# Gate norm, convolution, GELU and the product with up moved from the w_down stage into the Strassen stage, and four k tiles of w_out moved to its second part

## The chip, the cores and the metric

The kernel runs on one NeuronCore of one Trainium2 chip. The metric is the device time of one execution in microseconds, shown as the median of the runs, lower being better. The engines are TensorE (PE, with its weight loads as PEld), VectorE (DVE), ScalarE (ACT), GpSimd (POOL) and SyncE (SP). SP issues nearly all DMAs. Each engine works through its own queue strictly in order, and a semaphore wait of one instruction holds up all that stands behind it in that queue.

## The reference

One decoder layer on a (1, 512, 2048) float32 input. Three groups of attention heads feed one output projection; then a gated MLP with a causal depthwise convolution of width 3; then a gated per-layer embedding. The part that matters here:

```python
h = h + jnp.concatenate([oa, ob, oc], axis=-1) @ w_out[i]
c = rmsnorm(h, ffn_norm[i])
h = h + conv_ffn(c, w_gate[i], w_up[i], conv_w[i], conv_b[i], w_down[i])
e = rmsnorm(h, ple_norm[i])
h = h + jax.nn.sigmoid(e @ w_ple_gate[i]) * (p[i] @ w_ple_proj[i])

def conv_ffn(x, w_gate, w_up, conv_w, conv_b, w_down):
    hg = x @ w_gate                                  # (512, 5632)
    hg = causal_depthwise_conv(hg, conv_w, width=3) + conv_b
    return (jax.nn.gelu(hg, approximate=True) * (x @ w_up)) @ w_down
```

## The kernel before, in words

Every float32 matmul is done as three fp32r products. An operand is split into a high part (a cast on ACT, names ending in h) and a low part (a subtraction on DVE, names ending in l), and PE multiplies high by high, high by low and low by high. Weights come by DMA into `raw` tiles (three buffers), and `split_into` (lines 162 and 163 of the kernel) makes `wh` on ACT and `wl` on DVE (four buffers each).

The stages in order of time, each a list of groups that `run_groups` works through:

1. The input projection w_in, with the attention of the three head groups running beside it as background generators.
2. w_out in two parts. The four column blocks c = 0..3 (512 columns each) are first multiplied over 12 of the 16 k tiles (`order1`), and the result is added to x in `evac_o1` (line 1066). Then the four blocks are multiplied over the last four k tiles, and `evac_o2` (line 1071) adds these into `h` on DVE. The first part runs while the last attention unit is finished.
3. When a block c of `h` is complete, `operands(c)` transposes it on PE (line 1107), scales it on ACT (`T`, line 1108), and forms the seven Strassen operands of its k tiles on DVE (`st`, `sl`, lines 1116 and 1126) and ACT (`sh`, line 1121). `stats_store(c)` sums the squares on ACT (line 509) and stores `h` to DRAM. At the same time PE multiplies the second part of w_out for the next block and then w_ple_proj, the small product of the embedding (`evac_pp`).
4. The Strassen stage: 22 blocks of 256 columns of w_gate and 22 of w_up, taken in turn. A `Pair` is one such block. It takes seven products P1 to P7, each 8 k tiles by 3 matmuls of 256 columns, on PE lines 343 to 345. DVE forms weight differences (`T`, lines 238 to 248) and the `wl` splits and adds up results (lines 364, 367, 371); ACT makes the `wh` splits and copies results out of PSUM. `store_pair` then stores the two result tiles of the pair (128 x 512 each) to DRAM (`gu`).
5. w_down over 44 k tiles, in two passes: columns 0 to 1023, then 1024 to 2047. In the first pass `gated_load` loads the gate and up tiles of a k tile back, and `gated` makes its hidden tile: `z` = gate times the norm's scale on DVE (line 1207), the first tap with bias on ACT (line 1208), two more taps on DVE (lines 1210, 1213), GELU on ACT (line 1216), the product with up on DVE (line 1218). `hid_split` then makes `hh` on ACT (line 1227) and `hl` on DVE (line 1229). The 44 hidden tiles stay in SBUF for the second pass, which only splits them again.
6. w_ple_gate, and the output.

What sets the order: the program is recorded in the order in which the Python code calls it, with no scheduler behind it. Between pieces of PE work the code calls `tick()`, which advances every generator in the background list `bg` by one step. There are two ticks in each Strassen product and one after each bank of a group. `advance_split` puts the weight split of a product three places ahead of it. `need` functions run before a group or product and may tick until what they need has been recorded. All 512-column tiles of the background work share one pool of 69 pages; a page is used again when its last reader has finished.

Of the kernel before, what the change touches and what calls it, by code (L numbers as in the profile page):

```python
# [16 lines left out]
P = 128  # L17
# [35 lines left out]
def hybrid_layer_kernel(  # L53
# [142 lines left out]
    class Pair:  # L196


        def __init__(self, w, ct, dst):
            self.w, self.ct, self.dst = w, ct, dst  # L200
# [152 lines left out]
    def evac_product(p_, kind):  # L353
        m = T // 2
        x = p_.x[:, :m]
        if kind == "P1":
            p_.s = [page("ps") for _ in range(2)]
            p_.u = [page("pu") for _ in range(2)]
            p_.s1, p_.s2, p_.s3 = p_.s[0][:, :m], p_.s[0][:, m:], p_.s[1][:, :m]
            ACT.copy(p_.s1, x)  # L360
        elif kind == "P6":
            ACT.copy(p_.s2, x)
        elif kind == "P2":
            DVE.tensor_tensor(p_.u[0][:, :m], p_.y[:, :m], p_.s1, op=ALU.add)
        elif kind == "P7":
            ACT.copy(p_.s3, x)  # L366
            DVE.tensor_tensor(p_.u[1][:, m:], p_.z[:, :m], p_.s3, op=ALU.add)
        elif kind == "P4":
            ACT.copy(p_.u[0][:, m:], x)
        elif kind == "P3":  # L370
            DVE.tensor_tensor(p_.u[1][:, :m], p_.z[:, :m], p_.s2, op=ALU.add)
            bg.append(store_pair(p_))

    def store_pair(p_):
        for c in range(2):
            yield
            yield
            SP.dma_start(p_.dst(p_.ct + c), p_.u[c])
# [706 lines left out]
    def stats_store(c):  # L1085
        for t in range(NT):
            cT.stat(t, c, hp)
            yield
        while state.get("operands", -1) < c:
            yield  # L1090
        for t in range(NT):
            hd[t, c] = dpool.tile([P, NB], F32, tag=name("hd"), name=name("hd"))
            SP.dma_start(hd[t, c], hp[t][c])
        if c == 3:
            yield from cT.finish_gen(True)

# [84 lines left out]
    gd, ud = {}, {}  # L1181

    def pair_dst(d):
        def dst(ct):
            d[ct] = dpool.tile([P, T], F32, tag=name("gu"), name=name("gu"))
            return d[ct]
        return dst

    NC = D_FF // P
    cur = {"kt": -1}  # L1190
    gp = {}

    def gated_load():

        for kt in range(NC):
            while kt > cur["post"] + 2 or kt not in gd or kt not in ud:
                yield
            g, u = page("g"), page("u")
            SP.dma_start(g, gd[kt])
            SP.dma_start(u, ud[kt])  # L1200
            gp[kt] = g, u
            yield

    def gated(kt):
        g, u = gp.pop(kt)
        z = page("z")
        DVE.tensor_tensor(z, g, cT.rb, op=ALU.mult)
        ACT.activation(g, z, AF.Identity, scale=conv_col(2, kt), bias=conv_col(3, kt))  # L1208
        yield
        DVE.scalar_tensor_tensor(  # L1210
            g[:, 1:], z[:, : T - 1], conv_col(1, kt), g[:, 1:], op0=ALU.mult, op1=ALU.add
        )
        DVE.scalar_tensor_tensor(
            g[:, 2:], z[:, : T - 2], conv_col(0, kt), g[:, 2:], op0=ALU.mult, op1=ALU.add
        )
        ACT.activation(g, g, AF.Gelu_apprx_tanh)
        yield
        DVE.tensor_tensor(u, g, u, op=ALU.mult)
        hid_raw[kt] = u
        yield from hid_split(kt)  # L1220

    hid_raw = {}

    def hid_split(kt):
        u = hid_raw[kt]
# [5 lines left out]
        yield  # L1231

    def gated_all():
        for kt in range(NC):
            while kt > cur["kt"] + 4 or kt not in gp:
                yield
            cur["post"] = kt
            bg.append(gated(kt))
            yield
            yield  # L1240
            yield

    def split_all():
        for kt in range(NC):
            while kt > cur["kt"] + 4:
                yield
# [43 lines left out]
    def load_p():  # L1290
        pt = [page("p") for _ in range(2)]
# [16 lines left out]
    def evac_pp(c):  # L1308
        def evac(b, ps):
            t = xtile("b22")[:, :NB] if c < 2 else page("ppe")  # L1310
# [73 lines left out]
    order1 = [0, 1, 2, 3, 8, 9, 10, 11, 4, 5, 6, 7]  # L1384
    for c in range(4):
# [11 lines left out]
        groups.append(Group(2, w_out, krow, [(c * NB, NB)], mk, order1, evac_o1(c), need=need))  # L1397
    for c in range(4):
        need = None
        if c == 0:  # L1400
            need = once(lambda: (drain(units[2]["attn"]), open_xpool(), bg.append(conv_constants())))
        elif c == 2:
            need = once(lambda: bg.append(load_p()))
        groups.append(Group(2, w_out, krow, [(c * NB, NB)], mk, [12, 13, 14, 15], evac_o2(c), need=need))
# [5 lines left out]
    for q in range(NC // 2):  # L1410
        pairs.append(Pair(w_gate, 2 * q, pair_dst(gd)))
        pairs.append(Pair(w_up, 2 * q, pair_dst(ud)))
    order = [(0, "P1")]
    for r in range(len(pairs)):
        if r < len(pairs) - 1:
            order += [(r, "P5"), (r, "P6"), (r, "P2"), (r, "P7"), (r + 1, "P1"), (r, "P4"), (r, "P3")]
        else:
            order.insert(-1, (r, "P5"))
            order.insert(-1, (r, "P6"))
            order += [(r, "P7"), (r, "P2"), (r, "P4"), (r, "P3")]  # L1420
    for r, kind in order:
        if r < len(pairs):
# [5 lines left out]
            if (r, kind) == (len(pairs) - 1, "P6"):  # L1428
                def begin_down():
                    cur["post"] = -1  # L1430
                    bg.extend([gated_load(), gated_all()])
                c.need = begin_down

    for cs in ((0, 1), (2, 3)):
        def need(kts, cs=cs):
            if kts[0] == 0:
                cur["kt"] = -1
                if cs[0]:
                    hid.clear()
# [93 lines left out]
```

## Time and profile before

| | |
|---|---|
| median of 3 runs | 2585.02 us (2583.57 to 2585.78) |
| the profiled execution, its own time | 2583.13 us |
| its span, first to last instruction | 2581.4 us |
| PE busy | 2510.5 us, 97% of the span |
| DVE busy | 1441.8 us, 56% |
| ACT busy | 995.8 us, 39% |
| mean granted PE clock | 0.990 |

The profiled execution's time is 1.7 us above its span. Matmuls are pipelined, so that PE counts as busy whenever one is in flight; how many matmuls were done in a stretch of time says more of PE than its busy share. The stages begin at about 692 us (w_out, first part), 848 us (its second part), 906 us (w_ple_proj), 946 us (Strassen), 1837 us (w_down, first pass), 2147 us (second pass) and 2392 us (w_ple_gate). In the views of waits, "A <- B" says that engine A sat idle before its instruction until instruction B ended.

### The profile page before, as it was taken

To read this page: it belongs to the slowest core of one execution; us is meant where nothing else is said; L and a number is where in the kernel's file an instruction comes from. 1 tells how busy PE (TensorE), PEld (TensorE's weight loads), DVE (VectorE), ACT (ScalarE), POOL (GpSimd) and SP (SyncE) were. 2 spreads that over 40 slices of the span, in tenths; PEclk is the share of its full clock that TensorE was granted. 3 is DMA by queue.
4 is the path that set the end of the run, shared out by engine and by line. 5 is a ranking of instruction groups with operands and counts; after the bars stand their busy time and mean duration, and the time that the engine had idled before them with its cause. 6 is when DMAs were issued, how large, how long until landed. Compare 5 with 4: busy or idle time off the path is not lost.

```text
span 2581.4 us, 36548 instructions
## 1 busy us (share of the span) xinstructions
PE 2510.5 (97%) x14956; PEld 2210.9 (86%) x14956; DVE 1441.8 (56%) x1865; ACT 995.8 (39%) x1450; POOL 131.1 (5%) x232
## 2 busy tenths in 40 slices
PE   9999999999999889999999999999888889999999
PEld 7888898888888779999999999999766667888887
DVE  5253445445553577677777777677666664233433
ACT  5222244344432454444444444444444444222422
POOL 1132300101000000000000000000000000000000
PEclk9999999999999999999999999999899999999999
DMA  5322232232333354444444444444444453334342
GB/s 179 91 82 66 77 89 86 79 100 73 111 101 107 107 172 140 138 125 129 129 145 128 132 123 142 137 127 145 145 133 161 132 167 110 98 98 131 130 136 85
DMA packets 294180, 308.76 MB, mean 120 GB/s; under 512 B 12300, under 2 KB 207861, under 8 KB 294011
## 3 DMA queue, kind: packets, MB, share of 16 engines
q1 hardware_dynamic: 293978, 306.41, 38.6%
q8 instruction: 117, 1.92, 0.3%
q14 instruction: 53, 0.43, 0.1%
q10 hardware_dynamic: 32, 0.01, 0.0%
HBM read 270.70 MB, written 35.66 MB: 119 GB/s over the span
## 4 chain that ended last, share of the span: by engine, by line
PE 85%; DVE 7%; ACT 5%; issue 2%; DMA 0%; SPq 0%; ACTq 0%; DVEq 0%
PE g L313 13%; PE g L315 13%; PE g L314 12%; PE x L345 6%; PE x L343 6%; PE x L344 6%; PE m L345 5%; PE m L343 5%; PE m L344 5%; PE m L314 2%; PE m L315 2%; PE m L313 2%; DVE wl L163 1%; ACT g L1208 1%; ACT wh L162 1%
## 5 line engine op out<-in xcount | busy, mean ns | idle before, releaser
L163 DVE TENSOR_TENSOR wl<-raw,wh 128x1024 fp32r<-128x1024 f32 (+1 forms) x350 | 427.8, 1233 | 528.1 <-ACT wh L162 526.7
L162 ACT CAST wh<-raw 128x1024 fp32r<-128x1024 f32 (+1 forms) x350 | 360.5, 1042 | 537.8 <-PE g L315 385.9
L343 PE MATMUL x<-sh,wh 128*128 128x256 f32 x1408 | 398.8, 283 | 6.9 <-ACT ps L366 5.4
L313 PE MATMUL g<-wh,ah 128*128 128x512 f32 (+2 forms) x1024 | 398.4, 389 | 0.8 <-ACT ah L501 0.8
L345 PE MATMUL x<-sh,wl 128*128 128x256 f32 x1408 | 398.4, 283 | 0.0
L344 PE MATMUL x<-sl,wh 128*128 128x256 f32 x1408 | 397.6, 282 | 0.0
L315 PE MATMUL g<-wh,al 128*128 128x512 f32 (+2 forms) x1024 | 390.0, 381 | 0.0
L314 PE MATMUL g<-wl,ah 128*128 128x512 f32 (+2 forms) x1024 | 388.6, 379 | 0.0
L163 DVE TENSOR_TENSOR wl<-T,wh 128x1024 fp32r<-128x1024 f32 x176 | 215.4, 1224 | 158.3 <-ACT wh L162 158.3
L343 PE MATMUL m<-sh,wh 128*128 128x256 f32 x1056 | 298.1, 282 | 0.0
L345 PE MATMUL m<-sh,wl 128*128 128x256 f32 x1056 | 297.9, 282 | 0.0
L344 PE MATMUL m<-sl,wh 128*128 128x256 f32 x1056 | 297.4, 282 | 0.0
L343 PEld LDWEIGHTS x<-sh,wh 128*128 128x128 f32 x1408 | 268.7, 191 | 7.3 <-ACT ps L366 5.6
L345 PEld LDWEIGHTS x<-sh,wl 128*128 128x128 f32 x1408 | 268.9, 191 | 0.0
L344 PEld LDWEIGHTS x<-sl,wh 128*128 128x128 f32 x1408 | 268.8, 191 | 0.0
L315 PEld LDWEIGHTS g<-wh,al 128*128 128x128 f32 x1024 | 192.8, 188 | 38.9 <-DVE al L502 0.5
L314 PEld LDWEIGHTS g<-wl,ah 128*128 128x128 f32 x1024 | 193.5, 189 | 34.5
L313 PEld LDWEIGHTS g<-wh,ah 128*128 128x128 f32 x1024 | 193.4, 189 | 34.1 <-ACT ah L501 1.2
L162 ACT CAST wh<-T 128x1024 fp32r<-128x1024 f32 x176 | 184.9, 1051 | 64.3 <-PE m L344 61.4
L345 PEld LDWEIGHTS m<-sh,wl 128*128 128x128 f32 x1056 | 200.8, 190 | 0.0
L343 PEld LDWEIGHTS m<-sh,wh 128*128 128x128 f32 x1056 | 200.7, 190 | 0.0
L344 PEld LDWEIGHTS m<-sl,wh 128*128 128x128 f32 x1056 | 200.7, 190 | 0.0
(271 smaller groups left out, 3876.4 us busy)
## 6 DMA issues: line engine op xcount, KB each, us to landing
raw<-in_w_down_dram SPq DMA_DIRECT2D x88, 512.0 KB
raw<-in_w_in_dram SPq DMA_DIRECT2D x82, 512.0 KB
raw<-in_w_gate_dram SPq DMA_DIRECT2D x66, 512.0 KB
raw<-in_w_up_dram SPq DMA_DIRECT2D x66, 512.0 KB
gu<-pu SPq DMA_DIRECT2D x88, 256.0 KB
raw<-in_w_out_dram SPq DMA_DIRECT2D x32, 512.0 KB
raw<-in_w_ple_gate_dram SPq DMA_DIRECT2D x32, 512.0 KB
b<-in_w_gate_dram SPq DMA_DIRECT2D x22, 512.0 KB
```

The source lines that it names most:

```text
L162: ACT.copy(c.h[:, :m], src)
L163: DVE.tensor_tensor(c.l[:, :m], src, c.h[:, :m].bitcast(F32), op=ALU.subtract)
L313: PE.matmul(o, th, ch, start=st, stop=False)
L314: PE.matmul(o, th, cl, start=False, stop=False)
L315: PE.matmul(o, tl, ch, start=False, stop=sp)
L343: PE.matmul(ps, vh[:, k, :], ah, start=st and k == 0, stop=False, skip_group_check=not st)
L344: PE.matmul(ps, vh[:, k, :], al, start=False, stop=False, skip_group_check=not st)
L345: PE.matmul(ps, vl[:, k, :], ah, start=False, stop=k == 7, skip_group_check=not st)
L1208: ACT.activation(g, z, AF.Identity, scale=conv_col(2, kt), bias=conv_col(3, kt))
```

## The change

- The gate tiles no longer go to DRAM. When a gate pair is done, `gate_done` puts two steps for each of its two tiles on a list: `gate_norm` (`z` on DVE and the first tap on ACT) and `gate_conv` (two taps on DVE, GELU on ACT). When an up pair is done, `up_done` adds a step `hidden` for each tile: the product on DVE, and then a store of the finished hidden tile to DRAM (`hid`). The generator `step_all` does one step every four ticks, that is every two products, and one every tick once w_down has begun.
- w_down loads the hidden tile of each k tile from DRAM, in both passes, and splits it; the 44 tiles no longer stay in SBUF. The loads of the first pass begin at the last pair's P7.
- A pair takes one page for its partial sums in place of two.
- w_out: block 0 keeps 12 k tiles in the first part and 4 in the second; blocks 1 to 3 have 8 in each. `stats_store` does its sums and stores after the operands of the block. The tiles of p and the results of w_ple_proj lie in other buffers, and p is loaded one block later.

Three places show how the instructions moved. The first is DVE in the second part of w_out, where the sums of the block's last bank into `h` stand, for which the transposes wait (`st` and `sl` are the Strassen operands of the block before, `wl` a weight split). Before, from the third bank's sum of block 1 on:

```order
L1071 TENSOR_TENSOR h_5948<-g_7062,h_5948 128x512
L1116 TENSOR_TENSOR st_7110<-T_7012 128x512
L1126 TENSOR_TENSOR sl_7114<-T_7013,sh_7090 128x512
L1126 TENSOR_TENSOR sl_7118<-st_7110,sh_7112 128x512
L1116 TENSOR_TENSOR st_7120<-T_7013,st_7084 128x512
L1126 TENSOR_TENSOR sl_7124<-T_7013,sh_7116 128x512
L1126 TENSOR_TENSOR sl_7126<-st_7120,sh_7122 128x512
L163 TENSOR_TENSOR wl_7131<-raw_6948,wh_7130 128x1024
L1071 TENSOR_TENSOR h_5970<-g_7096,h_5970 128x512
```

After the change, the same block:

```order
L1120 TENSOR_TENSOR sl_6937<-st_6931,sh_6933 128x512
L163 TENSOR_TENSOR wl_6944<-raw_6768,wh_6943 128x1024
L163 TENSOR_TENSOR wl_6966<-raw_6816,wh_6965 128x1024
L1065 TENSOR_TENSOR h_5887<-g_6818,h_5887 128x512
L1065 TENSOR_TENSOR h_5922<-g_6852,h_5922 128x512
L1065 TENSOR_TENSOR h_5948<-g_6877,h_5948 128x512
L419 COPY cw_6758<-m_7001 128x88
L163 TENSOR_TENSOR wl_7022<-raw_6850,wh_7021 128x1024
L1065 TENSOR_TENSOR h_5970<-g_6908,h_5970 128x512
```

The operands of block 0 are now all ahead of the four sums of block 1, and only a weight split and a small copy stand between the last two sums.

The second place is DVE in the middle of the Strassen stage, from a sum of P3 on (`L371`) to the next product's difference. Before:

```order
L371 TENSOR_TENSOR pu_9827<-m_9864,ps_9824 128x256
L163 TENSOR_TENSOR wl_10120<-T_10087,wh_10119 128x1024
L248 TENSOR_TENSOR T_10021<-raw_9961,T_10021 128x1024
L163 TENSOR_TENSOR wl_10153<-raw_10027,wh_10152 128x1024
L163 TENSOR_TENSOR wl_10187<-T_10021,wh_10186 128x1024
L364 TENSOR_TENSOR pu_10055<-m_10158,ps_10053 128x256
L238 TENSOR_TENSOR T_10217<-raw_10123,raw_10027 128x1024
```

After the change, at such a place:

```order
L371 TENSOR_TENSOR pu_8845<-m_8720,ps_8683 128x256
L163 TENSOR_TENSOR wl_8980<-T_8947,wh_8979 128x1024
L1196 TENSOR_TENSOR z_8997<-pu_8844,rb 128x512
L248 TENSOR_TENSOR T_8883<-raw_8818,T_8883 128x1024
L163 TENSOR_TENSOR wl_9014<-raw_8889,wh_9013 128x1024
L163 TENSOR_TENSOR wl_9046<-T_8883,wh_9045 128x1024
L1201 SCALAR_TENSOR_TENSOR pu_8844<-z_8997,cw_6758,pu_8844 128x511
L1204 SCALAR_TENSOR_TENSOR pu_8844<-z_8997,cw_6758,pu_8844 128x510
L364 TENSOR_TENSOR pu_9078<-m_9019,ps_8915 128x256
L238 TENSOR_TENSOR T_9081<-raw_8983,raw_8889 128x1024
```

One step of the gate tile now stands between splits, two products apart from the next.

The third place is DVE in the first pass of w_down, two k tiles. Before:

```order
L163 TENSOR_TENSOR wl_18559<-raw_18460,wh_18558 128x1024
L1207 TENSOR_TENSOR z_18574<-g_18480,rb 128x512
L1210 SCALAR_TENSOR_TENSOR g_18480<-z_18574,cw_6938,g_18480 128x511
L1213 SCALAR_TENSOR_TENSOR g_18480<-z_18574,cw_6938,g_18480 128x510
L1218 TENSOR_TENSOR u_18481<-g_18480,u_18481 128x512
L1229 TENSOR_TENSOR hl_18594<-u_18481,hh_18593 128x512
L1207 TENSOR_TENSOR z_18607<-g_18512,rb 128x512
L1210 SCALAR_TENSOR_TENSOR g_18512<-z_18607,cw_6938,g_18512 128x511
L1213 SCALAR_TENSOR_TENSOR g_18512<-z_18607,cw_6938,g_18512 128x510
L1218 TENSOR_TENSOR u_18513<-g_18512,u_18513 128x512
L1229 TENSOR_TENSOR hl_18627<-u_18513,hh_18626 128x512
L163 TENSOR_TENSOR wl_18637<-raw_18472,wh_18636 128x1024
```

After the change:

```order
L163 TENSOR_TENSOR wl_18404<-raw_18275,wh_18403 128x1024
L163 TENSOR_TENSOR wl_18419<-raw_18335,wh_18418 128x1024
L1237 TENSOR_TENSOR hl_18416<-hid_18379,hh_18415 128x512
L1237 TENSOR_TENSOR hl_18460<-hid_18431,hh_18459 128x512
L163 TENSOR_TENSOR wl_18476<-raw_18350,wh_18475 128x1024
```

Eight of the instructions between two pairs of splits are gone; the two `hl` now read tiles that a DMA has loaded.

The diff, cut to its core:

```diff
@@ evac_product
         if kind == "P1":
-            p_.s = [page("ps") for _ in range(2)]
-            p_.u = [page("pu") for _ in range(2)]
-            p_.s1, p_.s2, p_.s3 = p_.s[0][:, :m], p_.s[0][:, m:], p_.s[1][:, :m]
+            s = page("ps")
+            p_.s1, p_.s2 = s[:, :m], s[:, m:]
...
         elif kind == "P3":
             DVE.tensor_tensor(p_.u[1][:, :m], p_.z[:, :m], p_.s2, op=ALU.add)
-            bg.append(store_pair(p_))
+            p_.done(p_)
@@ stats_store
+        while state.get("operands", -1) < c:
+            yield
         for t in range(NT):
             cT.stat(t, c, hp)
-            yield
-        while state.get("operands", -1) < c:
-            yield
-        for t in range(NT):
             hd[t, c] = dpool.tile([P, NB], F32, tag=name("hd"), name=name("hd"))
             SP.dma_start(hd[t, c], hp[t][c])
+            yield
         if c == 3:
             yield from cT.finish_gen(True)
+            state["rb"] = 1
@@ the gated part (gated_load, gated and gated_all are gone)
+    def gate_done(p_):
+        for i in range(2):
+            gates[p_.ct + i] = p_.u[i]
+            steps.append(lambda ct=p_.ct + i: gate_norm(ct))
+            steps.append(lambda ct=p_.ct + i: gate_conv(ct))
+
+    def up_done(p_):
+        for i in range(2):
+            steps.append(lambda ct=p_.ct + i, u=p_.u[i]: hidden(ct, u))
...
+    def hidden(ct, u):
+        DVE.tensor_tensor(u, gates.pop(ct), u, op=ALU.mult)
+        hdd[ct] = dpool.tile([P, T], F32, tag=name("hid"), name=name("hid"))
+        def store():
+            yield
+            SP.dma_start(hdd[ct], u)
+        after(store())
+
+    def step_all():
+        while "rb" not in state:
+            yield
+        while "down" not in state or steps:
+            if steps:
+                steps.pop(0)()
+            for _ in range(1 if "down" in state else 4):
+                yield
...
     def hid_split(kt):
-        u = hid_raw[kt]
+        u = page("hid")
+        SP.dma_start(u, hdd[kt])
+        for _ in range(4):
+            yield
         hh, hl = page("hh", F32R), page("hl", F32R)
...
     def split_all():
         for kt in range(NC):
-            while kt > cur["kt"] + 4:
+            while kt > cur["kt"] + 5 or kt not in hdd:
                 yield
@@ w_out
     order1 = [0, 1, 2, 3, 8, 9, 10, 11, 4, 5, 6, 7]
+    order2 = [4, 5, 6, 7, 12, 13, 14, 15]
...
-        groups.append(Group(2, w_out, krow, [(c * NB, NB)], mk, order1, evac_o1(c), need=need))
+        o = order1 if c == 0 else order1[:8]
+        groups.append(Group(2, w_out, krow, [(c * NB, NB)], mk, o, evac_o1(c), need=need))
...
-        groups.append(Group(2, w_out, krow, [(c * NB, NB)], mk, [12, 13, 14, 15], evac_o2(c), need=need))
+        o = order2[4:] if c == 0 else order2
+        groups.append(Group(2, w_out, krow, [(c * NB, NB)], mk, o, evac_o2(c), need=need))
@@ the Strassen order
+            if (r, kind) == (1, "P1"):
+                c.need = lambda: bg.append(step_all())
-            if (r, kind) == (len(pairs) - 1, "P6"):
+            if (r, kind) == (len(pairs) - 1, "P7"):
                 def begin_down():
-                    cur["post"] = -1
-                    bg.extend([gated_load(), gated_all()])
+                    cur["kt"] = -1
+                    bg.append(split_all())
```

More of the change, by code (lines that the diff above doesn't have):

```diff
@@ L363, in evac_product @@
         elif kind == "P2":
+            p_.u = [page("pu") for _ in range(2)]
             DVE.tensor_tensor(p_.u[0][:, :m], p_.y[:, :m], p_.s1, op=ALU.add)
         elif kind == "P7":
-            ACT.copy(p_.s3, x)
-            DVE.tensor_tensor(p_.u[1][:, m:], p_.z[:, :m], p_.s3, op=ALU.add)
+            ACT.copy(p_.s1, x)
+            DVE.tensor_tensor(p_.u[1][:, m:], p_.z[:, :m], p_.s1, op=ALU.add)
         elif kind == "P4":
@@ L1179, in conv_col @@
         return conv["w2b"][:, (k - 2) * n + ct : (k - 2) * n + ct + 1]
[L1181 to L1187, printed above, removed]
-    NC = D_FF // P
[L1190 to L1209, printed above, removed]
+    NC = D_FF // P
+    cur = {}
+    gates = {}
+    hdd = {}
+    steps = []
+    def gate_done(p_):
[3 more added lines that the diff above has]
+            steps.append(lambda ct=p_.ct + i: gate_conv(ct))
@@ L1210, in gated, with gate_norm, gate_conv @@
+    def up_done(p_):
+        for i in range(2):
+            steps.append(lambda ct=p_.ct + i, u=p_.u[i]: hidden(ct, u))
+    zs = {}
+    def gate_norm(ct):
+        zs[ct] = page("z")
+        g = gates[ct]
+        DVE.tensor_tensor(zs[ct], g, cT.rb, op=ALU.mult)
+        ACT.activation(g, zs[ct], AF.Identity, scale=conv_col(2, ct), bias=conv_col(3, ct))
+    def gate_conv(ct):
+        g, z = gates[ct], zs.pop(ct)
         DVE.scalar_tensor_tensor(
-            g[:, 1:], z[:, : T - 1], conv_col(1, kt), g[:, 1:], op0=ALU.mult, op1=ALU.add
+            g[:, 1:], z[:, : T - 1], conv_col(1, ct), g[:, 1:], op0=ALU.mult, op1=ALU.add
@@ L1212, in gated @@
         )
         DVE.scalar_tensor_tensor(
-            g[:, 2:], z[:, : T - 2], conv_col(0, kt), g[:, 2:], op0=ALU.mult, op1=ALU.add
+            g[:, 2:], z[:, : T - 2], conv_col(0, ct), g[:, 2:], op0=ALU.mult, op1=ALU.add
         )
         ACT.activation(g, g, AF.Gelu_apprx_tanh)
[L1217 to L1222, printed above, removed]
+    def hidden(ct, u):
[4 more added lines that the diff above has]
+            SP.dma_start(hdd[ct], u)
+            state["stored"] = ct
+        after(store())
@@ L1290, in load_p @@
     def load_p():
-        pt = [page("p") for _ in range(2)]
+        pt = xtile("b22").rearrange("p (k n) -> p k n", k=2)
+        pt = [pt[:, k, :] for k in range(2)]
         for t in range(NT):
@@ L1309, in evac @@
         def evac(b, ps):
-            t = xtile("b22")[:, :NB] if c < 2 else page("ppe")
+            if c == 3:
+                t = page("ppe")
+            else:
+                if b % 2 == 0:
+                    pp["t"] = xtile("b22" if c < 2 else "T")
+                t = pp["t"][:, b % 2 * NB : b % 2 * NB + NB]
             if b % 2 == 0:
@@ L1417, in hybrid_layer_kernel @@
         else:
-            order.insert(-1, (r, "P5"))
-            order.insert(-1, (r, "P6"))
-            order += [(r, "P7"), (r, "P2"), (r, "P4"), (r, "P3")]
+            for kind in ("P5", "P6", "P2", "P7"):
+                order.insert(-1, (r, kind))
+            order += [(r, "P4"), (r, "P3")]
     for r, kind in order:
```

39 lines of the change are left out of this document (14 added, 25 removed).

## The prediction, made before the result was known

> **What bounds the kernel now.** I read the page's fourth part first, then the stages side by side, then the waits of the stages in which PE falls behind.
>
> ```profile
> PE 85%; DVE 7%; ACT 5%; issue 2%; DMA 0%; SPq 0%; ACTq 0%; DVEq 0%
> ```
>
> PE makes up most of the chain that ended last, so time can be had where PE is not on it. The next view gives each stretch its length, then busy time and number of instructions of PE, PEld, DVE, ACT and POOL, the granted PE clock, the DMA share and GB/s.
>
> ```profile
> 848.00:906.00 58.00, 51.28 (x236) 41.55 (x236) 33.89 (x51) 29.92 (x58) 0.20 (x1) 0.94 0.35 109
> 906.00:946.00 40.00, 29.52 (x124) 22.83 (x123) 24.75 (x39) 20.01 (x39) 2.01 (x6) 0.91 0.52 177
> 1200.00:1500.00 300.00, 300.00 (x2520) 300.00 (x2519) 212.86 (x211) 126.60 (x165) 0.00 (x0) 1.00 0.44 132
> 2000.00:2100.00 100.00, 86.08 (x330) 63.93 (x329) 65.36 (x84) 42.00 (x56) 0.00 (x0) 0.95 0.45 148
> 2200.00:2300.00 100.00, 100.00 (x432) 80.73 (x432) 32.08 (x36) 27.38 (x36) 0.00 (x0) 1.00 0.31 95
> ```
>
> In 100 us the second pass of w_down (2200 to 2300) does 432 matmuls of 512 columns, or 0.2315 us each, at full clock; the first pass (2000 to 2100) does 330 of the same. The Strassen stage does 2520 of 256 columns in 300 us, 0.1190 each, without a gap. So PE bounds Strassen and the second pass; something else bounds the first pass, the end of Strassen, and the end of w_out.
>
> In the first pass it is a chain between DVE and ACT. Of the waits from 1837 to 2147 us, PE's for the low weight part, and then DVE in order of time (the bracket is its idle time before):
>
> ```profile
> PE m L314 <- DVE wl L163: 16.8, 33, 0.8
> 1876.37 2.36 DVE L163 TENSOR_TENSOR wl<-raw,wh 128x1024 fp32r<-128x1024 f32 x2 [0.26 <-ACT wh L162]
> 1878.64 0.68 DVE L1207 TENSOR_TENSOR z<-g,rb 128x512 f32<-128x512 f32 x1
> 1880.21 0.75 DVE L1210 SCALAR_TENSOR_TENSOR g<-z,cw,g 128x511 f32<-128x511 f32 x1 [0.88 <-ACT g L1208]
> 1883.88 0.69 DVE L1229 TENSOR_TENSOR hl<-u,hh 128x512 fp32r<-128x512 f32 x1 [0.69 <-ACT hh L1227]
> 1890.68 2.36 DVE L163 TENSOR_TENSOR wl<-raw,wh 128x1024 fp32r<-128x1024 f32 x2 [0.25 <-ACT wh L162]
> ```
>
> The cycle of two k tiles takes 1890.68 - 1876.37 = 14.31 us, while their 48 matmuls need 48 x 0.2315 = 11.1. Each step of a hidden tile waits for the other engine, the weight split stands behind two such tiles, and PE waits for that split, 33 times in 44 k tiles.
>
> **First pass of w_down: about -63 us.** It begins at 1837.1 and the second at 2146.88:
>
> ```profile
> L313 PE MATMUL m<-wh,hh x352: 387/392/796, 1837.1 to 2385.8; 128*128 128x512 f32 x176
> 2144.86 1.12 ACT L1227 CAST hh<-u 128x512 fp32r<-128x512 f32 x2
> 2146.88 0.40 PE L313 MATMUL m<-wh,hh 128*128 128x512 f32 x1
> ```
>
> That is 309.8 us for 44 x 8 x 3 = 1056 matmuls, whose floor is 1056 x 0.2315 = 244.4: 65.4 us too many. The change takes `z`, both taps and the product off DVE and two activations off ACT here, and leaves per k tile one `wl`, one `wh`, one `hl` and one `hh`, which is what the second pass has now (432 per 100 us). I keep 2 us for the first groups, where the steps of the last two gate tiles (two `z`, four taps, two products, 5.8 us of DVE) still stand among the splits: -63.
>
> What it adds here are 44 loads of 256 KB in place of 88. Per k tile the queue carries 512 KB of weights and 256 KB of hidden tile in 5.56 us, 141 GB/s; the row of 2000 to 2100 shows 148 carried. A load is recorded four ticks ahead of its `hh` copy, and the copy five k tiles ahead of its use, so a late landing first eats two and a half groups of 11.1 us. SP's weight loads stand in line with it, but with three `raw` buffers they too are more than a group ahead.
>
> **Gate work in Strassen: 0 us, from 0 to +66.**
>
> ```profile
> L1207 DVE TENSOR_TENSOR z<-g,rb 128x512 f32<-128x512 f32 x44 | 30.1, 685 | 0.0
> L1210 DVE SCALAR_TENSOR_TENSOR g<-z,cw,g 128x511 f32<-128x511 f32 x44 | 33.0, 751 | 36.8 <-ACT g L1208 36.8
> L1213 DVE SCALAR_TENSOR_TENSOR g<-z,cw,g 128x510 f32<-128x510 f32 x44 | 33.0, 750 | 1.6
> L1218 DVE TENSOR_TENSOR u<-g,u 128x512 f32<-128x512 f32 x44 | 30.5, 692 | 32.8 <-ACT g L1216 32.8
> L1208 ACT ACTIVATE g<-z,cw2b 128x512 f32<-128x512 f32 x44 | 35.9, 816 | 77.9 <-DVE z L1207 77.9
> L1216 ACT ACTIVATE g<-g 128x512 f32<-128x512 f32 x44 | 27.8, 632 | 72.4 <-DVE g L1213 72.4
> ```
>
> A gate pair and an up pair take 14 products of 24 x 0.1190 = 2.86 us, 40.0 us. DVE is busy 212.86 / 300 of that, 28.4 us; two tiles add 2 x (0.685 + 0.751 + 0.750 + 0.692) = 5.8, which makes 34.2, or 85%. ACT goes from 16.9 to 16.9 + 2 x (0.816 + 0.632) = 19.8, 49%. So both fit, if the order does not make PE wait. What hides the work is the lead of the splits:
>
> ```profile
> 1199.64 1.22 DVE L163 TENSOR_TENSOR wl<-b,wh 128x1024 fp32r<-128x1024 f32 x1
> 1209.61 0.42 DVE L371 TENSOR_TENSOR pu<-m,ps 128x256 f32<-128x256 f32 x1 [0.26 <-PE m L345]
> 1216.68 1.23 DVE L163 TENSOR_TENSOR wl<-T,wh 128x1024 fp32r<-128x1024 f32 x1 [1.96 <-ACT wh L162]
> ```
>
> The first row is P3's split, done at 1200.86. P3 itself ended just before its sum at 1209.61, so that it began at about 1206.7: 5.8 us after its split. The largest step is the two taps, 1.5 us, and the next comes two products (5.7 us) later; in between DVE now idles, 1.96 us at the third row and 87 of 300 us in all, so a delay does not pile up. ACT waits for `z` and for the taps inside its queue, with the next `wh` behind it, and this comes out of the same lead. On SP there is one store of 256 KB per hidden tile in place of two, and a weight load that waits for DVE to free its buffer comes later by at most a step. If the cover were gone, the taps of 44 tiles would stand on the path, 44 x 1.5 = 66 us; below nothing I see no way, since PE has no gap there. The rows are far nearer to 0.
>
> **The end of Strassen: about -8 us, from -11 to 0.** PE's 7392 matmuls begin at 946.3 and should take 880.0; the next stage's first matmul is at 1837.1, 10.8 us late.
>
> ```profile
> L343 PE MATMUL x<-sh,wh x1408: 278/283/582, 946.3 to 1833.4; 128*128 128x256 f32 x176
> 1827.80 0.62 ACT L1227 CAST hh<-u 128x512 fp32r<-128x512 f32 x1 [1.89 <-DVE u L1218]
> 1828.33 0.37 ACT L366 COPY ps<-x 128x256 f32<-128x256 f32 x1
> 1828.74 0.58 PE L343 MATMUL x<-sh,wh 128*128 128x256 f32 x1 [5.41 <-ACT ps L366]
> 1830.19 0.41 PE L343 MATMUL x<-sh,wh 128*128 128x256 f32 x1
> 1830.41 0.41 PE L344 MATMUL x<-sl,wh 128*128 128x256 f32 x1
> ```
>
> PE stands 5.41 us because the copy of P7 queues on ACT behind the first gated tiles, and then starts one matmul in 0.21 us rather than 0.12. After the change only casts of loaded tiles, and the activations of one gate tile, stand there. What is late next is the load of the second hidden tile, behind a weight load on SP: I keep 3 us.
>
> **The end of w_out: about -12 us, from -19 to -4.**
>
> ```profile
> PE m L1107 <- DVE h L1071: 11.5, 3, 4.8
> PE g L313 <- ACT b L1312: 2.9, 1, 2.9
> PE m L527 <- DVE dg L522: 2.6, 1, 2.6
> L1126 DVE TENSOR_TENSOR sl<-st,sh 128x512 fp32r<-128x512 f32 x16 | 11.0, 691 | 1.2 <-ACT sh L1121 0.2
> 880.53 1.03 PE L1107 MATMUL m<-ident,h 128*128 128x128 f32 x8
> 913.24 1.33 PE L1107 MATMUL m<-ident,h 128*128 128x128 f32 x5 [4.79 <-DVE h L1071]
> 914.79 0.63 PE L314 MATMUL g<-wl,ph 128*128 128x512 f32 x1
> 915.22 0.63 PE L315 MATMUL g<-wh,pl 128*128 128x512 f32 x1
> 916.38 0.39 PE L315 MATMUL g<-wh,pl 128*128 128x512 f32 x1
> ```
>
> The 98 us from 848 to 946 hold 288 matmuls (66.7 us) and some 72 transposes (eight in 1.03 us, so 9 us): 22 too many, 17 of them in these three waits. The transposes of blocks 1, 2 and 3 wait for the block's last sum, which stands on DVE behind the operands of the block before. Moving 12 x 4 x 3 = 144 matmuls, 33.3 us, from the first part into blocks 1 to 3 gives each block 22.2 us of PE work in place of 11.1, against 7.6 us of operands on DVE (four differences and seven low parts at 0.69), so these are done before the sum. All three waits go, 11.5 us, with three slow stretches of about 1.1 us each (five transposes and six matmuls from 913.24 to 916.38, 3.1 us, at full clock 2.0). I keep 2.4, half of block 3's wait, since w_ple_proj is as short as before: -12. The two smaller waits stay. If nothing came, -4 would be the wait of one block; if all went, -19.
>
> Here a rule of the skill weighs in. The Trainium skill, "TensorE: Matmul & The Clock Gate", section "What's actually happening", says that after too little work PE gets half its clock, until some 3.4 us of sustained work have passed. By it a slow stretch would cost 1.7 us rather than 1.1 and this term would be about -14; the rows above show a start every 0.42 us instead of 0.23, but for a shorter time.
>
> The moved matmuls also leave the first part with 33.3 us less cover for the last attention unit:
>
> ```profile
> L1003 PE MATMUL m<-pth,vl x48: 273/310/397, 411.9 to 806.4; 128*128 128x512 f32 x12, 128*128 128x384 f32 x12, 128*128 128x256 f32 x12, 128*128 128x128 f32 x12
> ```
>
> It ends at 806.4 and the second part begins at 848, so 8 us of margin remain. I take 0.
>
> **Between the passes: about +2 us, from 0 to +6.** PE goes straight into the second pass now, and the first two `hh` are cast at 2144.86 from SBUF. After the change two loads must land first, on SP behind the weight loads of the last groups and on ACT behind the sums of squares. With a lead of a few us I take 2.
>
> The table load for GELU moves into Strassen and lies in the lead. Pages and stores cost DVE nothing that PE sees.
>
> **Sum.** -63 + 0 - 8 - 12 + 2 = -81. The profiled execution took 2583.1 us, 1.7 above its span, so 2502 is expected of such an execution; the median lies 1.9 above it: 2504.
>
> **Rivals.**
>
> - *w_out gives nothing.* If pages or the attention's end hold up the second part, its -12 is lost: 2516. For it: 16 pages of mixed heads live on while the operands fill theirs. Against it: the margin of 8 us.
> - *Strassen pays.* ACT's waits for DVE and DVE's for ACT join, as they do in the first pass, and each gate tile costs PE its taps: 2504 + 66 = 2570. Against it: the lead of 5.8 us, four times a step.
> - *The steps do not get done.* 132 steps, one per two products, need 264 of 308 products; if they ran late, the first pass would keep its chain and about 2504 + 63 = 2567 would result. Against it: only the last two gate tiles are recorded behind the last product.
> - *The other side: the reload bounds both passes.* If a load lands later than the lead covers, ACT's `hh` waits in its queue with `wh` behind it, and both passes go at 14.3 us for two k tiles: 65 us lost again in the first and 65 new ones in the second, 2504 + 130 = 2634, slower by 49. It decides once a load takes some 11 us, a whole group, from issue to landing. For it: 141 GB/s must hold for 490 us. Against it: no wait of the first pass now names a DMA, with twice the number of loads.
>
> The same page of the Trainium skill, section "HAM oscillation — how this bites in real kernels", says that a wait for data in every k tile sends PE back to half clock each time. By that rule the last rival would be dearer still; the first pass as it is, with a wait in every group, shows a clock of 0.95.
>
> **How the numbers follow.** The forecast has 0.72, w_out's rival 0.12, Strassen's 0.08, the late steps 0.04, the reload 0.04. A change within 0.2% (5 us) is what a measurement of this kernel cannot tell from none; only a mixture would land there, 0.01, taken from the first three. Faster is then 0.95 and slower 0.04. The forecast's own range is the sum of the near bounds: -65 - 11 - 19 + 0 gives 2490, -60 - 4 - 4 + 6 gives 2523. It holds w_out's rival too; I take 2490 to 2530.
>
> **What would show it.** First pass of w_down: 430 or more matmuls per 100 us at clock 1.00, and no wait of PE for `wl` or `wh` but in its first 30 us; were there DMA releasers on `hh`, the reload rival would hold. Strassen: 2520 matmuls in 300 us, DVE at about 85%, and no row of PE waiting for a split; fewer than 2500 would speak for its rival. w_out: transposes with no wait for `h`, and Strassen's first product some 12 us earlier than 946.3. Between the passes: an idle of PE of a few us. The forecast is wrong if the first pass takes over 260 us or Strassen over 890.

## The result and the profile after

The changed kernel takes 2498.61 us (median of 4 runs, 2498.07 to 2499.42) against 2584.30 us for the kernel before on the same chip: a ratio of 0.967, with a 95% interval of 0.965 to 0.969. That is 85.7 us less; forecast were 81 less and 2504 us, in a range of 2490 to 2530. The profiled execution took 2498.18 us with a span of 2496.1. Two single executions of the groups below, 3472.39 us of the kernel before and 3016.68 us of the one with two loads a group earlier, had a mean granted clock of 0.65 and 0.75 and stand in no comparison.

Where the time went, stage by stage, from the first matmul of each in the two traces:

| stretch | before, us | after, us | difference | forecast |
|---|---|---|---|---|
| to Strassen's first product | 946.3 | 933.6 | -12.7 | -12 |
| Strassen, to w_down's first matmul | 890.8 | 882.3 | -8.5 | 0 and -8 |
| first pass of w_down | 309.8 | 245.2 | -64.6 | -63 |
| second pass to the end of the span | 434.5 | 435.0 | +0.4 | +2 |

The rows behind the boundaries of after (the second pass begins where the output banks are `m` again, as at 2146.88 before):

```profile
L343 PE MATMUL x<-sh,wh x1408: 279/283/322, 933.6 to 1812.7; 128*128 128x256 f32 x176
L313 PE MATMUL m<-wh,hh x352: 388/392/396, 1815.9 to 2300.1; 128*128 128x512 f32 x176
2061.15 0.40 PE L313 MATMUL m<-wh,hh 128*128 128x512 f32 x1
```

The stages of the changed kernel side by side, in the columns shown before (length; busy time and instructions of PE, PEld, DVE, ACT, POOL; granted clock, DMA share, GB/s):

```profile
860.00:900.00 40.00, 37.43 (x167) 30.04 (x167) 20.64 (x29) 17.73 (x35) 0.00 (x0) 0.96 0.40 125
900.00:934.00 34.00, 26.90 (x127) 20.58 (x126) 20.09 (x31) 18.62 (x33) 2.01 (x6) 1.00 0.53 178
1200.00:1500.00 300.00, 300.00 (x2520) 300.00 (x2519) 246.65 (x269) 143.80 (x195) 0.00 (x0) 1.00 0.39 116
2000.00:2100.00 100.00, 100.00 (x433) 80.73 (x432) 38.71 (x44) 33.47 (x52) 0.00 (x0) 1.00 0.51 163
```

Strassen still does 2520 matmuls in 300 us, with DVE at 82% in place of 71. The row from 2000 to 2100 lies across the end of the first pass, at 2061.1, and holds 433 matmuls, PE's floor. PE's waits in the whole span, as the view of waits lists them, are these (engine, line, what it waited for; us in total, times, longest):

```profile
PE g L313 <- ACT b L1315: 4.4, 2, 3.2
PE m L450 <- DMA ga<-in_attn_norm_dram: 3.9, 1, 3.9
PE m L1298 <- DMA b<-in_p_dram: 2.6, 1, 2.6
PE m L521 <- DVE dg L516: 1.4, 1, 1.4
PE m L1101 <- DVE h L1065: 1.2, 1, 1.2
PE m L345 <- DVE wl L163: 1.1, 1, 1.1
PE g L313 <- ACT ah L495: 1.0, 1, 1.0
```

Of before's list the 34.0 us for `wh` and `wl` in w_down are gone, and the 11.5 us of the transposes for `h` are 1.2. New is a wait of 2.6 us for the load of `p`. But a view of the same trace that the forecast had not asked for shows how the first pass now lives. These are the two largest waits of ACT from 1815 to 2061 us:

```profile
ACT hh L1235 <- DMA hid<-hid: 146.9, 23, 8.3
ACT wh L162 <- PE g L315: 16.4, 14, 9.0
```

In each group of two k tiles ACT stands some 7 us at the cast `hh` for the load of the hidden tile, 294.9 us in 44 places over both passes, and PE never notices. Why not, and how near it is, is the second question for the experiments.

### The profile page after: what moved, and what is told of

It reads as the page before. It is cut to its first block, busy times and chain, and to the rows that moved or that the text cites. A ratio compares the mean times of both kernels' runs of the same rounds, so it can differ in the third digit from the quotient of the medians.

```text
span 2496.1 us, 36419 instructions
## 1 busy us (share of the span) xinstructions
PE 2475.2 (99%) x14956; PEld 2197.2 (88%) x14956; DVE 1423.5 (57%) x1865; ACT 986.5 (40%) x1450; POOL 131.1 (5%) x232
## 4 chain that ended last, share of the span: by engine, by line
PE 98%; DMA 1%; DVE 1%; ACT 0%; issue 0%; SPq 0%; DVEq 0%
PE g L315 15%; PE g L313 15%; PE g L314 15%; PE x L345 7%; PE x L343 7%; PE x L344 7%; PE m L345 5%; PE m L343 5%; PE m L344 5%; PE m L314 3%; PE m L315 3%; PE m L313 3%; PE g L306 1%; PE g L308 1%; PE g L307 1%; PE m L648 1%
## 5 line engine op out<-in xcount | busy, mean ns | idle before, releaser
L1237 DVE TENSOR_TENSOR hl<-hid,hh 128x512 fp32r<-128x512 f32 x88 | 60.3, 688 | 246.6 <-ACT hh L1235 246.6
```

The costliest lines, as they stand in the source:

```text
L1237: DVE.tensor_tensor(hl, u, hh.bitcast(F32), op=ALU.subtract)
```

## The experiments

Times are compared with 2498.61 us for the changed kernel; kernels of one group ran on one chip beside the kernel before, whose median was 2584.60, 2584.98 and 2583.59 us in the three groups.

### Do the two halves add up, and what made w_out's gain?

**MLP alone** (w_out and the stores of its sums as before the change):

```diff
-        o = order1 if c == 0 else order1[:8]
-        groups.append(Group(2, w_out, krow, [(c * NB, NB)], mk, o, evac_o1(c), need=need))
+        groups.append(Group(2, w_out, krow, [(c * NB, NB)], mk, order1, evac_o1(c), need=need))
...
-        o = order2[4:] if c == 0 else order2
+        o = order2[4:]
```

> The changed kernel with w_out, its two parts and the stores of its sums as before the change (all twelve k tiles in the first part, four in the second, the sums of squares ahead of the operands). My theory, that the three waits of the transposes and the slow stretches behind them come back: 11 to 13 us over the changed kernel, so about 2510, with three waits of the transposes (L1101 or near it) for h of about 11 us in all. The rival that w_out gives nothing: within 3 us of the changed kernel.

Measured: 2511.82 us (2511.12 to 2513.37), 13.2 over the changed kernel. Its PE's waits and its windows:

```profile
PE m L1102 <- DVE h L1065: 11.1, 3, 4.7
...
860.00:900.00 40.00, 31.99 (x145) 25.49 (x145) 25.69 (x38) 23.80 (x47) 0.20 (x1) 0.92 0.36 117
900.00:934.00 34.00, 25.08 (x105) 19.51 (x104) 21.33 (x35) 19.17 (x39) 2.00 (x6) 0.85 0.31 105
```

The three waits for `h` are back with 11.1 us, and in the traces Strassen's first product comes 14.3 us later (947.9 against 933.6). The waits of the stretch together (with 2.9 for `b`, 1.6 for `p`, 1.2 each for `dg` and `wl` and 0.3 for Strassen's first product) are 18.3 us here and 10.7 in the changed kernel, 7.6 apart. The rest goes with the clock, 0.92 and 0.85 in the two windows against 0.96 and 1.00: over 40 and 34 us an estimated 1.6 and 5.1 us.

**w_out alone** (the kernel before, with the change to w_out and its loads and stores):

> The kernel before with the change to w_out alone (eight k tiles in blocks 1 to 3 of the second part, its loads and stores as changed), w_down as before. If the two halves of the change add up: before minus 11 to 13 us, about 2572. If the operands' stage only hides a wait that w_down then shows, or if the gain came from elsewhere: within 3 us of before.

Measured: 2572.61 us (2571.80 to 2574.04), 12.0 less than before. So the halves add up to within about a microsecond, 12 to 13 us for w_out and, 2584.60 - 2511.82, 72.8 us for the MLP, and the rival that w_out gives nothing falls.

**The sums of squares ahead of the operands again**, the matmuls as changed:

```diff
-        while state.get("operands", -1) < c:
-            yield
         for t in range(NT):
             cT.stat(t, c, hp)
+            yield
+        while state.get("operands", -1) < c:
+            yield
+        for t in range(NT):
```

> The changed kernel with one part of the w_out change undone: the sums of squares of a block again ahead of its operands, the matmuls as changed. My prediction put the whole gain on the moved matmuls: by it this is within 2 us of the changed kernel. The rival, that ACT's sums of squares (four of about 0.8 us a block) stood between a block and its operands and their move made part of the gain: 3 to 8 us slower.

Measured: 2503.55 us (2502.49 to 2503.98), 4.9 slower. The moved matmuls alone do end the long waits for `h`, but other waits grow:

```profile
PE m L1299 <- DMA b<-in_p_dram: 4.9, 1, 4.9
...
PE m L521 <- DVE dg L516: 2.7, 1, 2.7
PE m L1102 <- DVE h L1065: 1.2, 1, 1.2
```

The wait for the load of `p` is 2.3 us longer and that for `dg` 1.3, and 1.1 us at Strassen's first product is new; all waits of the stretch are 13.9 us in place of 10.7, since `b` falls from 4.4 to 2.9. In the traces Strassen's first product comes 5.9 us later (939.5), so nearly as much again, 2.7 us, is not a wait but goes with the clock: in the windows from 860 to 900 and from 900 to 934 it was 0.94 and 0.92 here, 0.96 and 1.00 as changed. SP's own timeline shows the load of `p`, of this kernel and then of the changed one:

```profile
872.04 17.53 SPq L181 DMA_DIRECT2D raw<-in_w_ple_proj_dram  x3
889.61 2.22 SPq L1087 DMA_DIRECT2D hd<-h  x4
891.88 2.75 SPq L1292 DMA_DIRECT2D b<-in_p_dram  x4
```

```profile
888.40 0.37 SPq L181 DMA_DIRECT2D raw<-in_w_ple_proj_dram  x1
888.82 0.46 SPq L1085 DMA_DIRECT2D hd<-h  x1
889.33 1.89 SPq L1291 DMA_DIRECT2D b<-in_p_dram  x4
```

With the sums first, all four stores of the third block's `h` are issued in a row ahead of `p`; as changed, one is. So some 5 of the 13 us are the sums' and stores' move, which the forecast had given no part, and some 8 are left for the moved matmuls.

**`p` loaded one group earlier.** Both fences also show what `p` stands behind: a weight load of w_ple_proj that waits for a free buffer until 888.

```diff
-            elif c == 3 and kts[0] == 12:
+            elif c == 3 and kts[0] == 4:
                 bg.append(load_p())
```

> The changed kernel with p loaded one group of four k tiles earlier (at the first half of the last block of w_out instead of the second). Its transposes wait 2.57 us for the load now, and PE starts at 0.37 us instead of 0.23 for some 2 us behind that: without the wait 3 to 4 us faster. If the next wait of the stage (3.17 us for a copy on ACT) takes the gain over: within 1 us of the changed kernel.

Measured: 2492.28 us (2492.10 to 2492.61), ratio to before 0.964 (0.963 to 0.966), 6.3 us less than the changed kernel: more than expected, and it beats both. SP issues `p` at 872.76, ahead of that weight load, and PE's waits between w_out and Strassen are now 0.5 us for `dg` and

```profile
PE g L313 <- ACT b L1315: 3.2, 1, 3.2
```

Not only `p`'s wait went, but the ones behind it too: 1.2 for `h`, the second of those for `b`, 0.9 of `dg`'s. Strassen's first product comes at 927.6.

**The last block's sums four ticks later**, on top of this:

```diff
+        for _ in range(4 if c == 3 else 0):
+            yield
         for t in range(NT):
             cT.stat(t, c, hp)
```

> The kernel with p loaded one group earlier, and the sums of squares of the last block of w_out put four ticks later, behind the copies of w_ple_proj on ACT. Two of them (0.8 us each) stand between the last operands and the copy for which PE waits 3.15 us there: about 1.6 us faster than with p's load alone, 2490 to 2491. If the wait is DVE's operands alone, or the later sums hold up the broadcast of the norm: no gain, 2492 to 2494.

Measured: 2495.02 us (2493.00 to 2496.31), 2.7 slower than with `p`'s load alone. The wait for `b` became two of some 2 us, and the broadcast of the norm was late:

```profile
PE g L313 <- ACT b L1317: 4.0, 2, 2.0
PE m L521 <- DVE dg L516: 3.1, 1, 3.1
...
914.72 0.58 ACT L1317 COPY b<-g 128x512 f32<-128x512 f32 x1 [5.88 <-DMA ppd<-b]
```

The last row, from its timeline, names what was next in line: the copy waits for the store of an earlier copy to free its buffer. Taking the sums away from ACT turned one wait into two.

### What covers the gate work in Strassen?

The forecast said: the 5.8 us by which a split is ahead of its product. Four edits set the steps against that lead, or against DVE's idle share.

**Six steps at once:**

```diff
-            if steps:
-                steps.pop(0)()
-            for _ in range(1 if "down" in state else 4):
+            for _ in range(1 if "down" in state else 6):
+                if steps:
+                    steps.pop(0)()
+            for _ in range(1 if "down" in state else 24):
                 yield
```

> The changed kernel with the six steps of a pair of hidden tiles recorded at one place, every twelve products, in place of one step every two products; the same work in all. My prediction costs the steps at nothing because a step (at most 1.5 us of DVE) is short against the 5.8 us by which a split is ahead of its product. The six are 5.8 us of DVE, and DVE waits for ACT some 3 us among them: PE stalls by about 3 us at each of 22 places, 50 to 70 us slower than the changed kernel. If what counts is only that DVE has 17% to spare, or the lead is longer than I read it: within 5 us.

Measured: 2587.42 us, 88.8 slower, as slow as before the change, with the same work on every engine. But PE does not wait mainly for the splits:

```profile
PE x L343 <- ACT ps L361: 25.4, 11, 4.9
PE x L343 <- ACT ps L366: 22.5, 6, 4.1
PE x L343 <- ACT wh L162: 3.7, 4, 0.9
PE x L345 <- DVE wl L163: 3.0, 4, 0.8
...
1200.00:1500.00 300.00, 280.02 (x2254) 278.39 (x2253) 226.71 (x244) 130.72 (x175) 0.00 (x0) 0.96 0.37 109
```

47.9 of these 54.6 us are for L361 and L366: ACT's copies of P6 and P7. The clock takes the rest: at 0.96 in place of 1.00 over the stage's 972 us it costs an estimated 39 us, and 54.6 and 39 are near the 88.8. These products gather in one bank with the next of their pair, so the copy must be done before that one begins, a product later. In the changed kernel's trace a copy of P6 starts at 1344.26, takes 0.37 and the next product of its bank starts at 1346.90:

```profile
1341.49 0.63 ACT L1207 ACTIVATE pu<-pu 128x512 f32<-128x512 f32 x1 [3.85 <-DVE pu L1204]
...
1344.26 0.37 ACT L361 COPY ps<-x 128x256 f32<-128x256 f32 x1 [0.24 <-PE x L345]
...
1346.90 0.28 PE L343 MATMUL x<-sh,wh 128*128 128x256 f32 x1
```

That is a margin of 1346.90 - 1344.63 = 2.27 us, not 5.8. And the first row is a GELU that held ACT for 3.85 us, longer than this margin; the copy was on time, by 0.24 us, since the whole wait and three casts fell between two copies. The next pair of runs tests that.

**A tile's norm and conv as one step, behind a copy** (two steps every eight ticks, begun three ticks later):

```diff
+        for _ in range(3):
+            yield
         while "down" not in state or steps:
-            if steps:
-                steps.pop(0)()
-            for _ in range(1 if "down" in state else 4):
+            for _ in range(1 if "down" in state else 2):
+                if steps:
+                    steps.pop(0)()
+            for _ in range(1 if "down" in state else 8):
                 yield
```

> The changed kernel with the norm and the conv of a gate tile recorded as one step, a step every four products, placed so that they stand on ACT right behind the copy of P6 or of P4. The chain of such a step (z 0.69, ACT's scaling 0.82, two taps 1.5, GELU 0.63, with what each waits) holds ACT some 4 to 6 us. New theory, from the run with six steps at once: what a step may delay is not the splits (5.8 us) but ACT's copies of P6 and P7, which must be done one product (2.86 us) after they can begin, a margin of 2.29 us. Here some two products pass between the step and the next such copy: 0 to 4 us slower than the changed kernel. By the splits' lead: 0 as well.

**The same, ahead of a copy** (begun six ticks later, the rest alike):

> The same steps three ticks (one and a half products) later, right ahead of P7's copy or one cast ahead of P6's, so that nothing lies between a step and the copy. New theory: the copy comes 3.5 to 5 us late against a margin of 2.29 us, so PE stands 1 to 3 us at 44 places: 40 to 110 us slower than the changed kernel, with waits of PE for the copies L361 and L366. By the splits' lead of 5.8 us, which my prediction held for the cover: within 5 us of the changed kernel, or PE waiting for wl.

Measured: 2500.22 us (2499.28 to 2500.65) behind a copy, 1.6 over the changed kernel, with 2520 matmuls in 300 us; 2524.54 us (2521.68 to 2526.05) ahead of one, 25.9 over. The same steps, a product and a half apart, differ by 24 us. The waits of the second, and one place of it:

```profile
PE x L343 <- ACT ps L366: 13.1, 11, 2.3
PE x L343 <- ACT ps L361: 6.7, 10, 0.7
...
1299.29 0.82 ACT L1197 ACTIVATE pu<-z,cw2b 128x512 f32<-128x512 f32 x1 [2.35 <-DVE z L1196]
1301.77 0.63 ACT L1207 ACTIVATE pu<-pu 128x512 f32<-128x512 f32 x1 [1.66 <-DVE pu L1204]
1302.31 0.35 ACT L366 COPY ps<-x 128x256 f32<-128x256 f32 x1
...
1302.71 0.39 PE L343 MATMUL x<-sh,wh 128*128 128x256 f32 x1 [1.07 <-ACT ps L366]
```

PE waits for nothing else in this stage but 1.0 us for its first `wl`; the list names 19.8 of the 25.9 us. At the place shown it was ready 1.07 us before 1302.71, so the copy was about 1.07 + 2.27 = 3.3 us late. The size was below what I had expected (40 to 110 us): only 21 of the 44 places show such a wait, and the copies of P6 came late by less, PE's waits for them being at most 0.7.

**One more DVE operation behind each step:**

```diff
                 steps.pop(0)()
+                if "down" not in state:
+                    for _ in range(1):
+                        DVE.tensor_tensor(page("junk"), cT.rb, cT.rb, op=ALU.mult)
```

> The changed kernel with one more product of 128x512 on DVE behind each of the 132 steps in Strassen, into a page that nothing reads: 132 x 0.685 = 90 us, which takes DVE from 82% to about 93% of that stage. If the lead covers the steps and DVE's share is what bounds it: within 5 us of the changed kernel, 2520 matmuls in 300 us. If the in-order waits between ACT and DVE had already used up the lead: 20 us or more slower, with waits of PE for the low part of the weights.

Measured: 2498.67 us (two executions), no change, and the window has all its matmuls with DVE at 90%:

```profile
1200.00:1500.00 300.00, 300.00 (x2520) 300.00 (x2519) 271.43 (x315) 145.78 (x196) 0.00 (x0) 1.00 0.40 118
```

So 90% of DVE costs nothing here. What decides is where ACT's waits stand against the copies.

### How near is the reload to the edge?

In one group of w_down in the changed kernel, from the timelines of SP, ACT and DVE:

```profile
1951.53 1.80 SPq L181 DMA_DIRECT2D raw<-in_w_down_dram  x2
1953.42 0.86 SPq L1231 DMA_DIRECT2D hid<-hid  x2
...
1959.21 0.62 ACT L1235 CAST hh<-hid 128x512 fp32r<-128x512 f32 x1 [7.50 <-DMA hid<-hid]
1960.34 1.05 ACT L162 CAST wh<-raw 128x1024 fp32r<-128x1024 f32 x1 [0.51 <-PE g L315]
...
1961.42 1.23 DVE L163 TENSOR_TENSOR wl<-raw,wh 128x1024 fp32r<-128x1024 f32 x1 [0.86 <-ACT wh L162]
1962.67 0.33 SPq L181 DMA_DIRECT2D raw<-in_w_down_dram  x1
```

This is a closed loop: a weight split frees a buffer, the next weight loads wait for that on SP, the hidden tiles' loads stand behind them and land 5.8 us after issue, `hh` waits for them on ACT, and the next weight split stands behind `hh`. It takes 1962.67 - 1951.53 = 11.14 us, of which 0.51 is a wait for PE: 10.6 us against PE's 11.11. The margin is half a microsecond.

**Each hidden tile loaded twice:**

```diff
         u = page("hid")
+        SP.dma_start(page("hx"), hdd[kt])
         SP.dma_start(u, hdd[kt])
```

> The changed kernel, but each hidden tile is loaded twice in w_down, first into a page that nothing reads: 256 KB and one issue of 0.43 us on SP more per k tile. My theory from the trace after: there is a closed loop of 10.6 us in each group of 11.1 us (the weight split on DVE frees a weight buffer, the weight load waits for that on SP, the loads of two hidden tiles stand behind it and land 5.8 us later, the cast hh waits for them on ACT, and the next weight split stands behind the cast). An extra load ahead of each makes the loop 12.5 to 14.5 us: 44 groups lose 1.4 to 3.4 us each, less a lead of some 20 us in each pass, so 25 to 110 us slower than the changed kernel. My prediction's reckoning (a late landing eats two and a half groups first, and a load decides only at some 11 us from issue to landing): within 5 us of the changed kernel.

**Twice, and a group earlier** (from the ninth k tile on):

```diff
-        for _ in range(4):
+        for _ in range(12 if kt >= 8 else 4):
             yield
...
-            while kt > cur["kt"] + 5 or kt not in hdd:
+            while kt > cur["kt"] + (7 if kt >= 8 else 5) or kt not in hdd:
```

> As the run with two loads of each hidden tile, with the loads of both recorded eight ticks (one group of 11.1 us) earlier from the ninth tile on, the casts where they were. If it is the loop's latency that cost time there, the loop is now two groups long and the loss goes: within 6 us of the changed kernel. If it is the bytes (a share of the DMA engines, 200 GB/s in place of 150), the loss stays.

**Three times** (`hx` and a second such page, `hy`, in front of `u`; casts and lead as changed):

> Two extra loads per hidden tile in w_down. From the trace of the run with one: a group of two k tiles took 11.35 us there in place of 11.11 (weight loads on SP at 1946.53, 1958.83, 1970.18, 1981.46), since the loop grew from 10.6 by some 0.75 us. A second extra load adds as much or, with more bytes at once, up to 1.5 us: a loop of 12.1 to 12.8, so 44 groups lose 1.0 to 1.7 us each, 44 to 75 us slower than the changed kernel. If the first extra load's 9 us were a cost by bytes and not by the loop: about 18 us.

Measured: 2507.59 us with two loads (+9.0), 2548.90 us with three (+50.3, 2543.81 to 2553.39). With two loads and a group's lead it is 2501.18 us, in one execution. The largest waits of ACT, and with three loads of PE, in w_down of the three, in that order:

```profile
ACT hh L1236 <- DMA hid<-hid: 338.1, 45, 9.5
```

```profile
ACT hh L1237 <- DMA hid<-hid: 372.4, 81, 10.7
PE m L314 <- DVE wl L163: 23.6, 37, 0.8
```

```profile
ACT wh L162 <- PE g L315: 303.1, 38, 9.1
ACT hh L1236 <- DMA hid<-hid: 31.1, 10, 8.8
```

From the start of its first matmul to that of the last with `wh` and `hh`, w_down takes 490.7 us as changed (1815.9 to 2306.6), 498.8 with two loads, 536.5 with three: 11.15, 11.34 and 12.19 us for each of 44 groups. The third moves along the line that the loop's lengthening gave (44 to 75 us more), and not by another 9 us. With the lead a group longer the same extra bytes (DMA share 0.61 in place of 0.48 over w_down) cost 2.0 us (492.7), and ACT's wait for loads falls from 338 to 31 us; it waits for PE instead. So the loop's latency costs most of the time, not the bytes; the run with the lead is a single execution. My estimate for two loads (25 to 110) was too high: in two groups in a row the first hidden tile's load, issued at 1948.90 and 1961.21, released its cast at 1955.97 and 1967.32, so 7.1 and 6.1 us later, and the loop passed PE's 11.11 us by only 0.2.

## Why the prediction was right, and where its steps were not

- **First pass of w_down, -63:** -64.6. The stage had been bound by the chain of DVE and ACT, and without it PE runs within a microsecond of its floor: 245.2 us against 244.4. Of the 2 us kept for the first groups 0.8 was needed, at most.
- **Gate work in Strassen, 0:** the number held, the cover named for it did not. "What hides the work is the lead of the splits" failed: the tightest cover is the 2.27 us margin of ACT's copies of P6 and P7, and a step holds ACT up to 4.5 us. What makes the term 0 is that a step falls every second product, at places of the cycle of 14 where no such copy follows too soon; for single steps that is read from the one place shown, since only joined steps were moved. So the 0 was in part luck: the forecast had not looked at these copies. Moved by a product and a half, two joined steps cost 24 us; all six together 89, more than the 66 given for a lost cover. DVE's idle share, the other argument, was sound: 90% cost nothing.
- **The end of Strassen, -8:** -8.5; w_down begins 2.3 us late in place of 10.8.
- **The end of w_out, -12:** -12.7 in the trace, -13.2 and -12.0 by taking w_out's change out of the changed kernel and by putting it alone into the one before. "All three waits go, 11.5 us" was nearly so (1.2 left, 2.4 kept), but "the two smaller waits stay" did not: `b` rose from 2.9 to 4.4, `dg` fell from 2.6 to 1.4, and a wait for `p` of 2.6 came, 2.9 us more in all. The slow stretches were mis-sized the other way. The clock was 0.50 in four stretches of 3.4 us before, from 875.3, 895.8, 912.8 and 933.3 on, and in one after, from 894.7 on. By the clock such a stretch costs about 1.7 us and not the 1.1 read from a part of it, the other size that the forecast named, and three fewer give an estimated 5.1 in place of 3.3. The step that was missing is the move of the sums and stores, which I had costed at nothing: 4.9 us of the gain, with 2.3 us of wait for `p`, whose load stood behind the stores on SP. The matmuls' move alone gave some 8 us, so that 12 came out is in part luck.
- **Between the passes, +2:** PE has no wait there, and the second pass to the end of the span took 0.4 us longer.
- **The reload.** The rival did not come true, but its threshold was wrong. "A late landing first eats two and a half groups" and "it decides once a load takes some 11 us" both overlook that the loads stand behind weight loads that wait for the very splits which stand behind the loads' casts: a lead that is recorded in ticks is worth nothing inside such a loop. With one load, 5.8 us from issue to cast, the reload is hidden; two loads cost 9 us, three 50. And "were there DMA releasers on `hh`, the reload rival would hold" was a false sign: there are 44 of them, 294.9 us, and PE waits for none.

The forecast cited the Trainium skill, "TensorE: Matmul & The Clock Gate", section "HAM oscillation — how this bites in real kernels", for a wait in every k tile that brings PE back to half clock. The page's example has waits of 3 to 5 us. With three loads PE waited in most groups, nearly always at most 0.8 us, and the granted clock was 1.00 in the windows of w_down; with six steps at once, where waits reached 4.9 us, it was 0.96, and behind each of Strassen's 13 waits of 2.9 us or more there is a stretch at 0.50 that begins during the wait or at most 1.2 us after it. The trace agrees with the page for waits of its size, and the forecast carried its rule too far.

## What to carry to other kernels

Look for the tightest consumer of an engine that is to take on waits, not for its idle share: an in-order queue with a margin of 2.3 us took steps of 4.5 us for nothing or for 24 us, by where they stood. Where a load waits on a queue behind another that needs a buffer freed by work behind the first, add up the loop and compare it with the period; what helped here was a whole period more of lead. A transfer that is needed soon must not stand behind a load that waits for a buffer: moving four small loads one group ahead was worth 6.3 us.

## What the runs showed of the hardware that I had not expected

The granted clock of a window is a mean of two values. In every trace of this case the records of the clock hold only 1.00 and 0.50, and each stretch at 0.50, but for the last, at the kernel's end, is 3.4 us long or two or three times that. The slow stretch behind the third wait for `h` before, of which the prediction shows the matmuls from 913.24 to 916.38, is one:

```profile
912.83:916.23 3.40, 2.99 (x10) 2.60 (x11) 0.36 (x1) 2.31 (x5) 0.00 (x0) 0.50 0.59 161
```

Short waits do not lower the granted clock alike. In the first pass before, waits of at most 1.5 us, but for one, left PE with 330 matmuls in 100 us at 0.95, which is three stretches of 3.4 us at 0.50. With three loads, waits of mostly at most 0.8 us left it with 376 in the window from 2200 to 2300 us at 1.00:

```profile
2200.00:2300.00 100.00, 91.41 (x376) 69.23 (x375) 29.01 (x32) 24.17 (x32) 0.00 (x0) 1.00 0.64 210
```

With the steps ahead of a copy, 21 waits of up to 2.3 us, spread over 907 us of Strassen, left the clock at 1.00 throughout. Whether the length of a wait, its distance from the next or PE's share decides was not tried.
